# The first layer of a four-layer trunk: maxima moved ahead on VectorE, products with v in one piece, fewer mask operations, weight splits tied to the units

## The chip, the cores and the metric

One core of a Trainium2 chip runs the whole program. The metric is the device time of one execution in microseconds (us), from runs of the kernel on the chip. The engines are called PE (TensorE, matrix products; PEld is its weight load), DVE (VectorE), ACT (ScalarE), POOL (GpSimd) and SP (SyncE, which issues DMAs).

## The reference

A trunk of four layers over x, 256 tokens of width 1024, in float32. Each layer normalises its input, mixes tokens in its own way, gates, projects and adds the normalised result. The first layer is native sparse attention with 16 query heads in 4 groups, and only that layer is touched here:

```python
q, kc, vc, ks, vs, kw, vw, gl, z = split_cols(u @ w_in, A_SPLITS)
p_c = masked_softmax(einsum(qb, kcmp) - slopes * dist, dist >= 0)   # 15 compressed keys
o_c = einsum(p_c, vcmp)
p_s = masked_softmax(einsum(qb, ksel) - slopes * dist, dist >= 0)   # selected blocks
p_w = masked_softmax(einsum(qb, kwin) - slopes * dist, mask)        # window
o = sum(gates * stack([o_c, o_s, o_w]))
return (o * silu(z)) @ w_out
```

With 256 tokens the selection takes all four blocks and the window covers everything, so both branches are causal softmax over all keys.

## The kernel before, in words

**Weights.** All weight matrices come through one list, `seq`, of 512 KB pieces. `advance` (L69) issues their loads on SP's queue into five raw buffers and splits each piece in two: ACT writes `whi`, a rounded copy (L104), and DVE `wlo`, the rest (L106). Each projection step is then three matmuls (hi with hi, lo with hi, hi with lo: L200 to L202). There are 11 buffer pairs (`NH`). A piece is freed after its eight steps and `advance` is called again, so a new piece is split when one is freed. Splits are ranked 250 places later than their place in the program (`LATE`). `st["after"]` holds instructions behind which the splits must be issued on their engine, and `st["most"]` is an upper limit on the piece to be split.

**Order.** PE's order is written by hand. On the other engines the compile step picks the order by rank, with `tc.high_priority(offset=...)` moving an instruction ahead by so many places (negative: back); an engine then executes its instructions in that fixed order. `evac`, the copy from PSUM, has `EARLY` = 80.

**The units of the first layer.** Eight units (`nsa_unit`, L767), each for two query heads, run in a pipeline (`pipeline`, L368). A unit's front is `scores_of(0, (0, 1))`, `scores_of(1, (0,))` and `finish`; its back, run among the front of the next unit, is two sets of transposes (`trans`) and two sets of products with v (`pv`). Even units begin with `cmp_front`, the compressed branch of a group, and its transposes (`cmp_back`) come in the next unit. After each slot `fill` runs some projection steps, so that 97 of them (the rest of q, and z) are spread over the slots: two per slot as long as more steps than slots remain, then one. Eight are kept for the end.

**In a unit.** Scores go to two PSUM buffers `S` (L785, L786). `softmax` (L293) adds the mask and takes the row maximum in one DVE instruction (L294, which releases the score buffer), and ACT takes the exponential (L296). In `finish` the row sums are inverted (L797) and times the gate (L800), and DVE scales the eight blocks of weights (L806, L807). PE transposes them (L301), ACT copies them out of PSUM (L146), and PE multiplies with v in 64-column halves (L317, L320); the compressed products (L819) follow behind the second set, then the copy of `o` (L144 or L146). `cmp_front` takes a third use of the `S` buffers (L736), reduces it (L740), adds the mask in four operations (L743), multiplies by slopes in two (L746), and goes on through maximum, exponential and sum (L749 to L758).

Of the kernel before, what the change touches and what calls it, by code (L numbers as in the profile page):

```python
# [15 lines left out]
OP = mybir.AluOpType  # L16
# [6 lines left out]
BIG = 3e38  # L23
NH, NS = 11, 5
LATE, LATEZ, EARLY = -250, -60, 80
# [12 lines left out]
def trunk(ctx, tc, I, out):  # L38
    nc = tc.nc
    PE, ACT, DVE, POOL = nc.tensor, nc.scalar, nc.vector, nc.gpsimd  # L40
# [9 lines left out]
    seq = []  # L50
# [15 lines left out]
    st = {"load": 0, "split": 0, "next": 0, "held": 0, "parts": 0, "after": [], "most": len(seq)}  # L66
# [71 lines left out]
    def evac(dst, src, eng=None):  # L138
        if eng is None:
            eng = "va"[cnt["ev"] % 2]  # L140
            cnt["ev"] += 1
        with tc.high_priority(offset=EARLY):
            if eng == "v":
                DVE.tensor_copy(dst, src)  # L144
            else:
                ACT.activation(dst, src, AF.Copy)  # L146
# [144 lines left out]
        return v  # L291

    def softmax(S, mask, slope, c0, c1, P, mx, l):  # L293
        DVE.tensor_tensor_reduce(out=P[:, c0:c1], in0=S, in1=mask[:, c0:c1], scale=-slope, scalar=BIG,  # L294
                                 op0=OP.add, op1=OP.min, accum_out=mx)
        ACT.activation(P[:, c0:c1], P[:, c0:c1], AF.Exp, bias=mx, scale=-1.0, accum_out=l)  # L296

    def transpose_p(P, eng=None):
        pt = ps.tile([128, 4, 128], F32, name="pt", bufs=2)
# [68 lines left out]
    def pipeline(units, ga, pattern, keep=8, tail=3):  # L368

        n = len(units)  # L370
        order = []
        for i in range(n + 1):
            f = list(units[i][0]) if i < n else [lambda: None] * tail
            b = list(units[i - 1][1]) if i else []
            for x in pattern:
                src = f if x == "F" else b
                if src:
                    order.append(src.pop(0))
            order += f + b
            if i == n - 1:  # L380
                order.append(ga.open)
        plan["slots"], plan["keep"] = len(order), keep
        for f in order:
            f()
            fill()
        drain()
        assert ga.ready == 4
        return ga.gh
# [160 lines left out]
    causal = [mask_tile("causal") for _ in range(2)]  # L549
# [3 lines left out]
    SLA = slopes_of(16)  # L553
# [6 lines left out]
    slc = const.tile([128, 4, 4], F32, name="slc")  # L560
    for hd in range(16):
        POOL.memset(slc[:, hd // 4, hd % 4:hd % 4 + 1], SLA[4 * (hd // 4) + hd % 2])
    dcmp = const.tile([128, 2, 2, 15], F32, name="dcmp")
    d0 = dcmp[:, 0]
    POOL.iota(d0, pattern=[[-128, 2], [16, 15]], base=31, channel_multiplier=-1,
              allow_small_or_imprecise_dtypes=True)
    POOL.affine_select(out=d0, in_=d0, pattern=[[128, 2], [-16, 15]], base=-31, channel_multiplier=1,
                       fill=NEG, compare_op=OP.is_ge)
    POOL.tensor_scalar(dcmp[:, 1], d0, 0.5, None, op0=OP.mult)
    bm = const.tile([60, 4], F32, name="bm")  # L570
    POOL.memset(bm, 0.5)
    POOL.affine_select(out=bm, in_=bm, pattern=[[-15, 4]], base=0, channel_multiplier=1, fill=0.0,
# [75 lines left out]
    t = {}  # L648
# [22 lines left out]
    def hidden_t():  # L671
# [7 lines left out]
        for k in range(2):  # L679
# [3 lines left out]
    vbd = [v[0:60, g // 2, 512 + 256 * (g % 2):768 + 256 * (g % 2)].rearrange("p (a d) -> p a d", a=4)  # L683
           for g in range(4)]
# [20 lines left out]
    n = st["next"]  # L705
# [17 lines left out]
    qT = t["q"]  # L723

    ga = Gate(0.5, silu_tanh)
    ga.push()
    CS, PTC = {}, {}

    def cmp_front(g):

        need(g)
        sc = ps.tile([128, 512], F32, name="S", bufs=NSB)
        for b in range(2):
            for a in range(4):
                c0 = (b * 4 + a) * 32
                PE.matmul(sc[:, c0:c0 + 32], qT[:, 4 * g + a, b * 128:(b + 1) * 128],  # L736
                          kc[:, g].rearrange("p a b -> p (a b)"), start=True, stop=True)
        cs = CS[g] = work.tile([128, 2, 4, 15], F32, name="cs", bufs=2)
        two = sc[:, 0:256].rearrange("p (a s n) -> p a n s", s=2, n=16)[:, :, 0:15, :]
        DVE.tensor_reduce(out=cs.rearrange("p b a n -> p (b a) n"), in_=two, axis=AX.X, op=OP.add)  # L740
        for b in range(2):
            for c in range(2):
                DVE.tensor_tensor(cs[:, b, 2 * c:2 * c + 2], cs[:, b, 2 * c:2 * c + 2],  # L743
                                  dcmp[:, c, b, None, :].to_broadcast([128, 2, 15]), op=OP.add)
        for b in range(2):
            DVE.tensor_tensor(cs[:, b], cs[:, b], slc[:, g, :, None].to_broadcast([128, 4, 15]), op=OP.mult)  # L746
        cs8 = cs.rearrange("p b a n -> p (b a) n")
        cm, cl = small(8, "cm", 2), small(8, "cl", 2)
        DVE.tensor_reduce(out=cm, in_=cs8, axis=AX.X, op=OP.max)  # L749
        DVE.tensor_scalar(cm, cm, -1e20, None, op0=OP.max)  # L750
        DVE.tensor_tensor(cs8, cs8, cm[:, :, None].to_broadcast([128, 8, 15]), op=OP.subtract)
        ACT.activation(cs, cs, AF.Exp)
        DVE.tensor_reduce(out=cl, in_=cs8, axis=AX.X, op=OP.add)
        DVE.tensor_scalar(cl, cl, 1e-30, None, op0=OP.max)
        DVE.reciprocal(cl, cl)
        DVE.tensor_tensor(cl.rearrange("p (b a) -> p b a", b=2), cl.rearrange("p (b a) -> p b a", b=2),
                          gate[:, :, 4 * g:4 * g + 4], op=OP.mult)
        DVE.tensor_tensor(cs8, cs8, cl[:, :, None].to_broadcast([128, 8, 15]), op=OP.mult)  # L758
# [8 lines left out]
    def nsa_unit(p):  # L767
        g, i = divmod(p, 2)
        t = {}

        def start():
            need(g)
            t["P"] = {(j, br): work.tile([128, 384], F32, name="P", bufs=8) for j in range(2) for br in range(2)}
            t["l"], t["mx"] = small(8, "la", 3), small(8, "mxa", 3)

        def scores_of(b, js):
            if b == 0:
                start()
            n = 128 * (b + 1)
            S = {}  # L780
            for j in js:
                s = ps.tile([128, 512], F32, name="S", bufs=NSB)
                s = s[:, 0:2 * n].rearrange("p (a n) -> p a n", a=2)
                q = qT[:, 2 * p + j, b * 128:(b + 1) * 128]
                PE.matmul(s, q, KH[:, g, :, 0:n], start=True, stop=False)  # L785
                PE.matmul(s, q, KL[g // 2][:, g % 2, :, 0:n], start=False, stop=True)  # L786
                S[j] = s
            for j in js:
                for br in range(2):
                    x = (j * 2 + br) * 2 + b  # L790
                    softmax(S[j][:, br, :], causal[i], SLA[4 * g + j], 128 * b, 128 * b + n, t["P"][j, br],
                            t["mx"][:, x:x + 1], t["l"][:, x:x + 1])

        def finish():
            scores_of(1, (1,))
            l = t["l"]
            DVE.reciprocal(l, l)  # L797
            gv = bass.AP(tensor=gate.tensor, offset=gate.offset + 16 + 2 * p,
                         ap=[list(gate.ap[0]), [1, 2], [16, 2], [48, 2]])
            DVE.tensor_tensor(l.rearrange("p (j r b) -> p j r b", j=2, r=2),  # L800
                              l.rearrange("p (j r b) -> p j r b", j=2, r=2), gv, op=OP.mult)
            for br in range(2):
                for j in range(2):
                    x = (j * 2 + br) * 2
                    P = t["P"][j, br]
                    DVE.tensor_scalar(P[:, 0:128], P[:, 0:128], l[:, x:x + 1], None, op0=OP.mult)  # L806
                    DVE.tensor_scalar(P[:, 128:384], P[:, 128:384], l[:, x + 1:x + 2], None, op0=OP.mult)  # L807

        def trans(br):
            t["PT", br] = [transpose_p(t["P"][j, br], "a") for j in range(2)]  # L810

        def pv(br):
            if br == 0:
                t["o"] = ps.tile([128, 256], F32, name="o", bufs=1)
            o = t["o"]
            pv_pair(o, t["PT", br], v, (br * 256 + g * 64,) * 2, br == 0, False)
            if br == 1:
                for j in range(2):
                    PE.matmul(o[64 * j:64 * j + 64, :], vbd[g][:, 2 * i + j, :], PTC[g], start=False, stop=True)  # L819
                evac(ga.oT[:, p, :], o)  # L820
                ga.have_o(p)

        front = [lambda: scores_of(0, (0, 1)), lambda: scores_of(1, (0,)), finish]
        back = [lambda: trans(0), lambda: trans(1), lambda: pv(0), lambda: pv(1)]
        if i == 0:
            front.insert(0, lambda: cmp_front(g))
            back.insert(0, lambda: cmp_back(g))
        return front, back

    trans = out_proj(pipeline([nsa_unit(p) for p in range(8)], ga, "FFBFBBB"), 0)  # L830


    SLB = slopes_of(8)
# [10 lines left out]
    for i in range(2):  # L844
        DVE.tensor_tensor_reduce(out=ljunk, in0=lamt[:, 2 * i, :], in1=lamt[:, 2 * i + 1, :], scale=1.0,
                                 scalar=0.0, op0=OP.mult, op1=OP.add, accum_out=lam[:, i:i + 1])
# [24 lines left out]
    ga = Gate(0.5, silu_tanh)  # L871
# [280 lines left out]
```

## Time and profile before

| | us |
|---|---|
| median of 3 runs (lowest to highest) | 589.78 (587.52 to 589.93) |
| the profiled execution, its own time | 592.12 |
| its span, first to last instruction | 590.4 |
| PE busy, share of the span | 568.9, 96% |
| DVE busy | 420.6, 71% |
| ACT busy | 334.8, 57% |
| POOL busy | 40.7, 7% |

The profile's times are microseconds from the start of the span. A busy PE is not PE at its peak, as matmuls are pipelined. The share of an engine is a mean over stages that differ: the four layers each have a stage of attention units with projections between, and a stage of projections alone. The units of the first layer run from about 72 to 165 us.

### The profile page before, as it was taken

The numbers are of one execution on the slowest core, as the hardware profiler recorded it, in microseconds if no ns is written. First come the engines' busy times: TensorE is split into PE (matmuls) and PEld (weight loads), VectorE is DVE, ScalarE is ACT, GpSimd is POOL, SyncE is SP. The second block draws the span as 40 slices with busy tenths as digits, with TensorE's granted clock in tenths as the row PEclk, the third lists the DMA queues.
The fourth block names the chain that finished last, engine by engine and source line by source line (L and its number), as shares of the span: only waits on it lengthen the run. The fifth ranks groups of instructions, "written<-read, shape, count | busy, mean of one in ns | idle before, by whom it ended". The sixth has DMA issues, their size and how long they took to land.

```text
span 590.4 us, 10479 instructions
## 1 busy us (share of the span) xinstructions
PE 568.9 (96%) x3930; PEld 502.5 (85%) x3930; DVE 420.6 (71%) x947; ACT 334.8 (57%) x715; POOL 40.7 (7%) x89
## 2 busy tenths in 40 slices
PE   7999987999999999999999999999999999999995
PEld 6998876777788799999988789998987898998984
DVE  5983898877836886777965885656748768888622
ACT  5742787767825575577633473555724655756410
POOL 1900000000000100000410100000001000000000
PEclk9999998989999999999999999999999999999998
DMA  8774825521250596443451587433434683342012
GB/s 284 243 256 143 314 79 191 170 70 40 78 171 11 180 331 235 144 143 108 143 167 48 179 295 267 143 116 105 146 107 147 223 314 137 117 134 73 1 37 72
DMA packets 27779, 90.96 MB, mean 154 GB/s; under 512 B 4560, under 2 KB 5200, under 8 KB 27728
## 3 DMA queue, kind: packets, MB, share of 16 engines
q1 hardware_dynamic: 26144, 86.09, 42.9%
q10 hardware_dynamic: 1584, 4.20, 2.2%
q8 instruction: 31, 0.51, 0.4%
q14 instruction: 20, 0.16, 0.1%
HBM read 89.22 MB, written 1.05 MB: 153 GB/s over the span
## 4 chain that ended last, share of the span: by engine, by line
PE 81%; DVE 9%; issue 4%; ACT 2%; DMA 2%; POOL 1%; SPq 0%; POOLq 0%; DVEq 0%; ACTq 0%
PE mm L200 15%; PE mm L201 14%; PE mm L202 14%; PE mm L260 6%; PE mm L262 6%; PE mm L261 6%; PE S L311 4%; PE pt L301 3%; DVE wlo L106 3%; PE o L317 2%; PE o L655 1%; DVE P L294 1%; ACT whi L104 1%; DMA h<-in_x_dram 1%; PE pt L188 1%
## 5 line engine op out<-in xcount | busy, mean ns | idle before, releaser
L200 PE MATMUL mm<-uth,whi 128*128 128x256 f32 x736 | 219.8, 299 | 0.0
L106 DVE TENSOR_TENSOR wlo<-raw,whi 128x1024 fp32r<-128x1024 f32 (+1 forms) x153 | 182.2, 1206 | 42.8 <-ACT whi L104 42.1
L201 PE MATMUL mm<-utl,whi 128*128 128x256 f32 x736 | 208.4, 283 | 0.0
L202 PE MATMUL mm<-uth,wlo 128*128 128x256 f32 x736 | 208.2, 283 | 0.0
L104 ACT ACTIVATE whi<-raw 128x1024 fp32r<-128x1024 f32 (+1 forms) x153 | 157.3, 1045 | 82.3 <-PE mm L201 50.0
L200 PEld LDWEIGHTS mm<-uth,whi 128*128 128x128 f32 x736 | 141.0, 192 | 17.5 <-issue 16.7
L201 PEld LDWEIGHTS mm<-utl,whi 128*128 128x128 f32 x736 | 141.4, 192 | 0.9
L202 PEld LDWEIGHTS mm<-uth,wlo 128*128 128x128 f32 x736 | 141.0, 192 | 0.0
L260 PE MATMUL mm<-whi,qT 128*128 128x512 f32 x128 | 50.4, 394 | 0.0
L261 PE MATMUL mm<-whi,kT 128*128 128x512 f32 x128 | 49.9, 390 | 0.0
L262 PE MATMUL mm<-wlo,qT 128*128 128x512 f32 x128 | 49.9, 390 | 0.0
L260 PE MATMUL mm<-whi,uth 128*128 128x512 f32 (+1 forms) x112 | 42.5, 380 | 0.0
L262 PE MATMUL mm<-wlo,uth 128*128 128x512 f32 (+1 forms) x112 | 42.1, 376 | 0.0
L261 PE MATMUL mm<-whi,utl 128*128 128x512 f32 (+1 forms) x112 | 42.0, 375 | 0.0
L294 DVE CUSTOM_DVE_ANT_0 P<-S,mask 128x128 f32<-128x128 f32 (+1 forms) x96 | 30.6, 353 | 8.4 <-PE S L786 6.2
L415 ACT ACTIVATE junk<-mm 128x512 bf16<-128x512 f32 x16 | 9.5, 595 | 42.1 <-PE mm L262 42.1
L296 ACT ACTIVATE P<-P,mxa 128x128 f32<-128x128 f32 (+1 forms) x64 | 28.5, 448 | 4.1 <-DVE mxa L294 4.1
L146 ACT ACTIVATE PT<-pt 128x384 f32<-128x384 f32 x58 | 26.1, 484 | 8.2 <-PE pt L301 7.9
L301 PE MATMUL pt<-ident,P 128*128 128x128 f32 x180 | 28.0, 286 | 0.5 <-DVE P L806 0.4
L262 PEld LDWEIGHTS mm<-wlo,qT 128*128 128x128 f32 x128 | 24.0, 188 | 5.1
L260 PEld LDWEIGHTS mm<-whi,qT 128*128 128x128 f32 x128 | 24.1, 188 | 4.7
L261 PEld LDWEIGHTS mm<-whi,kT 128*128 128x128 f32 x128 | 24.1, 188 | 4.6
(207 smaller groups left out, 768.8 us busy)
## 6 DMA issues: line engine op xcount, KB each, us to landing
raw<-in_a_t_dram SPq DMA_DIRECT2D x24, 512.0 KB, 4.9
raw<-in_b_t_dram SPq DMA_DIRECT2D x24, 512.0 KB, 4.6
raw<-in_d_t_dram SPq DMA_DIRECT2D x24, 512.0 KB, 4.8
raw<-in_c_t_dram SPq DMA_DIRECT2D x20, 512.0 KB, 4.6
raw<-in_w_dram SPq DMA_DIRECT2D x8, 512.0 KB, 4.8
raw<-in_a_o_dram SPq DMA_DIRECT2D x8, 512.0 KB, 3.5
raw<-in_b_v_dram SPq DMA_DIRECT2D x8, 512.0 KB, 3.5
raw<-in_b_o_dram SPq DMA_DIRECT2D x8, 512.0 KB, 3.5
```

Source lines behind the costliest of these rows:

```text
L104: ACT.activation(hi, t, AF.Copy)
L106: lo_of = (POOL if on_pool else DVE).tensor_tensor(lo, t, hi.bitcast(F32), op=OP.subtract)
L146: ACT.activation(dst, src, AF.Copy)
L200: PE.matmul(o, sh, mh, start=first, stop=False)
L201: PE.matmul(o, sh, ml, start=False, stop=False)
L202: PE.matmul(o, sl, mh, start=False, stop=last)
L260: PE.matmul(o, sh, wh[:, j, c0:c1], start=k == 0, stop=False)
L261: PE.matmul(o, sl, wh[:, j, c0:c1], start=False, stop=False)
L262: PE.matmul(o, sh, wl[:, j, c0:c1], start=False, stop=k == 7)
L294: DVE.tensor_tensor_reduce(out=P[:, c0:c1], in0=S, in1=mask[:, c0:c1], scale=-slope, scalar=BIG, op0=OP.add, op1=OP.min, accum_out=mx)
L296: ACT.activation(P[:, c0:c1], P[:, c0:c1], AF.Exp, bias=mx, scale=-1.0, accum_out=l)
L301: PE.transpose(pt[:, i, :], P[:, i * 128:(i + 1) * 128], ident)
```

## The change

- `softmax` returns its DVE instruction. In the first layer it is called with `EARLY`, so the maximum and the exponential rank 80 places earlier.
- The two sets of products with v become one slot, `pvs`, with the compressed products behind; the pattern of the slots loses a B.
- The mask of the compressed branch is stored in another order of its axes, and four additions and two multiplications become one of each, over 120 columns.
- `finish` sets `st["after"]` to its last maximum, raises the limit on pieces to be split and calls `advance`. The limit starts at 42 and is 42 + 2p after unit p; after the last unit there is none.

```diff
     def softmax(S, mask, slope, c0, c1, P, mx, l):
-        DVE.tensor_tensor_reduce(out=P[:, c0:c1], in0=S, in1=mask[:, c0:c1], scale=-slope, scalar=BIG,
-                                 op0=OP.add, op1=OP.min, accum_out=mx)
+        top = DVE.tensor_tensor_reduce(out=P[:, c0:c1], in0=S, in1=mask[:, c0:c1], scale=-slope, scalar=BIG,
+                                       op0=OP.add, op1=OP.min, accum_out=mx)
         ACT.activation(P[:, c0:c1], P[:, c0:c1], AF.Exp, bias=mx, scale=-1.0, accum_out=l)
+        return top.ins
...
     ga = Gate(0.5, silu_tanh)
+    PACE = st["most"] = st["next"] + 2
     ga.push()
...
-        for b in range(2):
-            for c in range(2):
-                DVE.tensor_tensor(cs[:, b, 2 * c:2 * c + 2], cs[:, b, 2 * c:2 * c + 2],
-                                  dcmp[:, c, b, None, :].to_broadcast([128, 2, 15]), op=OP.add)
-        for b in range(2):
-            DVE.tensor_tensor(cs[:, b], cs[:, b], slc[:, g, :, None].to_broadcast([128, 4, 15]), op=OP.mult)
+        pairs = cs.rearrange("p b (c j) n -> p (b c) j n", j=2)
+        DVE.tensor_tensor(pairs, pairs, dcmp.rearrange("p b c n -> p (b c) n")[:, :, None, :]
+                          .to_broadcast([128, 4, 2, 15]), op=OP.add)
+        DVE.tensor_tensor(cs, cs, slc[:, g, None, :, None].to_broadcast([128, 2, 4, 15]), op=OP.mult)
...
-                    softmax(S[j][:, br, :], causal[i], SLA[4 * g + j], 128 * b, 128 * b + n, t["P"][j, br],
-                            t["mx"][:, x:x + 1], t["l"][:, x:x + 1])
+                    with tc.high_priority(offset=EARLY):
+                        st["max"] = softmax(S[j][:, br, :], causal[i], SLA[4 * g + j], 128 * b, 128 * b + n,
+                                            t["P"][j, br], t["mx"][:, x:x + 1], t["l"][:, x:x + 1])
 
         def finish():
             scores_of(1, (1,))
+            st["after"], st["most"] = [st["max"]], PACE + 2 * p if p < 7 else len(seq)
+            advance()
...
-            if br == 1:
-                for j in range(2):
-                    PE.matmul(o[64 * j:64 * j + 64, :], vbd[g][:, 2 * i + j, :], PTC[g], start=False, stop=True)
-                evac(ga.oT[:, p, :], o)
-                ga.have_o(p)
+
+        def pvs():
+            pv(0)
+            pv(1)
+            o = t["o"]
+            for j in range(2):
+                PE.matmul(o[64 * j:64 * j + 64, :], vbd[g][:, 2 * i + j, :], PTC[g], start=False, stop=True)
+            evac(ga.oT[:, p, :], o)
+            ga.have_o(p)
...
-        back = [lambda: trans(0), lambda: trans(1), lambda: pv(0), lambda: pv(1)]
+        back = [lambda: trans(0), lambda: trans(1), pvs]
...
-    trans = out_proj(pipeline([nsa_unit(p) for p in range(8)], ga, "FFBFBBB"), 0)
+    trans = out_proj(pipeline([nsa_unit(p) for p in range(8)], ga, "FFBFBB"), 0)
+    st["after"] = []
```

## Rows read from the trace of the kernel before

**Rows 1.** The page, busy time of each engine, its share and instructions.
```profile
PE 568.9 (96%) x3930; PEld 502.5 (85%) x3930; DVE 420.6 (71%) x947; ACT 334.8 (57%) x715; POOL 40.7 (7%) x89
```

**Rows 2.** Windows; busy per engine (PE, PEld, DVE, ACT, POOL), clock, DMA.
```profile
70.00:110.00 40.00, 33.74 (x253) 29.30 (x251) 35.98 (x131) 31.36 (x82) 0.00 (x0) 0.96 0.47 159
110.00:125.00 15.00, 13.82 (x99) 11.84 (x97) 12.74 (x57) 10.18 (x32) 0.00 (x0) 0.89 0.32 107
125.00:165.00 40.00, 38.84 (x296) 30.19 (x295) 30.83 (x133) 29.12 (x91) 1.16 (x4) 1.00 0.22 70
...
100.00:105.00 5.00, 5.00 (x34) 4.34 (x35) 4.18 (x10) 3.92 (x10) 0.00 (x0) 0.74 0.41 121
120.00:125.00 5.00, 4.88 (x28) 4.77 (x28) 3.58 (x26) 3.05 (x12) 0.00 (x0) 0.69 0.01 4
```

**Rows 3.** PE's timeline, score products and a transpose; brackets: idle before, releaser.
```profile
75.63 0.47 PE L785 MATMUL S<-kT,qT 128*128 128x512 f32 x1 [1.49 <-DVE cm L750]
...
77.54 0.47 PE L785 MATMUL S<-kT,qT 128*128 128x512 f32 x1 [0.51 <-DVE cl L754]
...
93.34 0.39 PE L785 MATMUL S<-kT,qT 128*128 128x256 f32 x1 [0.93 <-DVE cs L740]
...
98.70 0.47 PE L785 MATMUL S<-kT,qT 128*128 128x512 f32 x1 [2.78 <-DVE cm L750]
...
120.12 0.58 PE L785 MATMUL S<-kT,qT 128*128 128x256 f32 x1 [1.09 <-DVE cs L740]
...
133.16 1.05 PE L301 MATMUL pt<-ident,P 128*128 128x128 f32 x5 [0.21 <-DVE P L806]
```

**Rows 4.** DVE's timeline ahead of PE's longest stall.
```profile
92.89 0.40 DVE L740 TENSOR_REDUCE cs<-S 128x120 f32<-128x240 f32 x1
...
95.94 1.23 DVE L106 TENSOR_TENSOR wlo<-raw,whi 128x1024 fp32r<-128x1024 f32 x1
97.09 0.48 DVE L743 TENSOR_TENSOR cs<-cs,dcmp 128x30 f32<-128x30 f32 x4
...
97.86 0.29 DVE L294 CUSTOM_DVE_ANT_0 P<-S,mask 128x128 f32<-128x128 f32 x1
...
98.27 0.28 DVE L294 CUSTOM_DVE_ANT_0 P<-S,mask 128x128 f32<-128x128 f32 x1
```

**Rows 5.** PE's timeline, the products with v of units 2 and 5.
```profile
114.20 0.65 PE L317 MATMUL o<-PT,v 128*64 128x256 f32 x4
...
144.09 0.65 PE L317 MATMUL o<-PT,v 128*64 128x256 f32 x4
...
144.89 0.39 PE L200 MATMUL mm<-uth,whi 128*128 128x256 f32 x1
145.11 0.28 PE L201 MATMUL mm<-utl,whi 128*128 128x256 f32 x1
145.23 0.28 PE L202 MATMUL mm<-uth,wlo 128*128 128x256 f32 x1
145.44 0.65 PE L317 MATMUL o<-PT,v 128*64 128x256 f32 x4
...
146.24 0.65 PE L819 MATMUL o<-PTc,v 60*64 60x256 f32 x4
```

**Rows 6.** ACT's timeline, an exponential and the last copy of transposed weights.
```profile
114.02 0.50 ACT L296 ACTIVATE P<-P,mxa 128x256 f32<-128x256 f32 x1
...
114.52 0.48 ACT L146 ACTIVATE PT<-pt 128x384 f32<-128x384 f32 x1
```

**Rows 7.** DVE's timeline ahead of the scalings of unit 3.
```profile
117.05 0.43 DVE L144 COPY oT<-o 128x256 f32<-128x256 f32 x1 [0.77 <-PE o L819]
```

**Rows 8.** Groups by line and shape, DVE, 71 to 165 us; xcount, busy us, mean ns.
```profile
L106 DVE TENSOR_TENSOR wlo<-raw,whi 128x1024 fp32r<-128x1024 f32 x18 | 21.6, 1214 | 0.0
L294 DVE CUSTOM_DVE_ANT_0 P<-S,mask 128x256 f32<-128x256 f32 x32 | 12.7, 416 | 4.5 <-PE S L786 4.5
...
L751 DVE TENSOR_TENSOR cs<-cs,cm 128x120 f32<-128x120 f32 x4 | 1.1, 280 | 0.0
```

More of the change, by code (lines that the diff above doesn't have):

```diff
@@ L563, in trunk @@
     dcmp = const.tile([128, 2, 2, 15], F32, name="dcmp")
-    d0 = dcmp[:, 0]
+    d0 = dcmp[:, :, 0]
     POOL.iota(d0, pattern=[[-128, 2], [16, 15]], base=31, channel_multiplier=-1,
@@ L568, in trunk @@
                        fill=NEG, compare_op=OP.is_ge)
-    POOL.tensor_scalar(dcmp[:, 1], d0, 0.5, None, op0=OP.mult)
+    POOL.tensor_scalar(dcmp[:, :, 1], d0, 0.5, None, op0=OP.mult)
     bm = const.tile([60, 4], F32, name="bm")
```

## The prediction

> **What bounds the kernel now.** I began with the page's busy shares: PE is busy for 568.9 of 590.4 us [rows 1], so all that a change off PE can give back is the 21.5 us in which PE stands still, the stretches in which PE's clock is halved, and work that PE does needlessly. Next I cut the stage that the diff touches, the eight units of the first layer (70 to 165 us), into windows [rows 2]. The reader is to see three regimes. From 70 to 110 PE is busy for 33.74 of 40 us while DVE is busy for 35.98: DVE has no room, and PE pays. From 110 to 125 PE loses 1.18 us, and the mean clock is 0.89. From 125 on PE is busy for 38.84 of 40 at a clock of 1.00, so there is about 1 us left to win. The clock has two levels here, 2.4 and 1.2 GHz, and a mean of 0.74 or 0.69 over 5 us [rows 2] means lost work of 0.26 x 5 = 1.3 us and 0.31 x 5 = 1.55 us. Both stretches come right behind a stall of PE.
>
> Then PE's timeline: the stalls of this stage are waits of the score products (L785) for a free score buffer [rows 3]. There are two such buffers; one comes free when both maxima that read it (L294) are through, or, behind the compressed products, when the reduction L740 is. DVE's own timeline shows why the longest stall (2.78 us, until 98.70) lasts so long [rows 4]: L740 frees the second buffer at 93.3 and the products of this unit's scores follow from 93.34 on [rows 3], but their maxima stand in DVE's queue behind eight scalings of the unit before (L806/L807), a q split (L644), a weight split (L106 at 95.94, 1.23 us) and six mask operations (L743/L746 from 97.09); the first runs at 97.86, the second at 98.27, and PE goes on at 98.70. PE's row names L750 as releaser, a tiny operation that stands between the maxima.
>
> **The change, part by part.**
>
> Products with v. pv(1) now follows pv(0) with no projection steps between. At 144.09 the first product starts, at 144.89 a projection step, at 145.44 the second product, whose successor L819 starts at 146.24 [rows 5]. A product set thus takes 0.80, and the gap of 1.35 between the two starts is 0.80 plus 0.55 for three matmuls; at full pace they take 0.36, as 256-column matmuls follow each other by 0.12 (145.11 and 145.23). So 0.19 us is the price of going from 64-column to 128-column work and back. All eight units pay it: 8 x 0.19 = **1.5 us** of PE, which nothing hides. The steps themselves move elsewhere.
>
> Fillers. The order has 60 slots instead of 68, for the same 97 projection steps, 8 of them kept back. Counted through, the units get 8, 14, 14, 14, 11, 7, 7, 8 (and 6 behind the last) instead of 8, 16, 16, 9, 8, 8, 8, 9 (7): unit 3, the one ahead of the second half-clock stretch, gains five steps. PE's total is the same; I put nothing on it.
>
> Pacing. Pieces 42 and later may now be split only when a unit's finish has raised the limit. Counted through the code this never binds: with 11 buffers, piece 42 can't be split before the 33rd projection step, in unit 2, when the limit is 44 already; 43 comes in unit 3 under 46, and so on. What is left is that the DVE half of a split is ordered behind the last maximum of the latest finished unit. It is an order on one queue, without a new semaphore, and the split already stands 250 places late. Cost and gain 0; no DMA is moved, and SP's and POOL's queues keep their order. If it did delay a split, eleven pieces of cover stand ahead of it.
>
> Mask operations. Six become two, four times. The six take 0.77 us (97.09 to 97.86 [rows 4]). A 128x120 operation of this kind (L751) has 280 ns [rows 8], so two of them take 0.56 at the most, and some 0.4 if they overlap as the six do (estimate). That frees 4 x 0.37 = 1.5 us of DVE. Once the maxima go first it is on no path of PE: 0, with 1.5 as the far end.
>
> Maxima first. Maximum and exponential rank 80 places earlier, ahead of scalings, q splits and mask operations.
> - Unit 0: stalls of 1.49 and 0.51 [rows 3]. Two maxima and one tiny operation take 0.41 (97.86 to 98.27 [rows 4]), so four in a row are through in some 0.85, while PE has two projection steps (0.72) to run before it asks. I take 2.0; bounds 0 and 2.0.
> - Unit 2: the stall of 2.78 [rows 3] goes, since the maxima no longer wait until 97.86, and with it the half clock behind it, 1.3 [rows 2]: 4.1. The 0.93 before it waits for L740, which keeps its rank: 0 taken, 0.93 as far end.
> - Unit 4: 1.09 [rows 3], again L740, which stands behind the scalings of unit 3, and these behind a copy for which DVE waited 0.77 [rows 7]; then 1.55 of half clock. The scalings of unit 3 can come earlier when their maxima do, but the copy may still block them: half of 2.6, **1.3**; bounds 0 and 2.6.
> - From unit 4's end on PE's waits are a few tenths each, 1.16 in all from 125 to 165 [rows 2], with DVE idle: they stay.
>
> What gets late instead: the scalings. In units 1, 3, 5 and 7 the transposes of the unit before follow finish directly, and in unit 5 PE already waits 0.21 for a scaling [rows 3]. Two 256-column maxima ahead of them are up to 2 x 0.42 = 0.83 [rows 8]. On ACT the exponentials (0.50) get ahead of the copies of the transposed weights; the last copy of unit 2 starts at 114.52 and ends at 115.00 [rows 6], which is just when the joined second product would start (114.20 + 0.80 [rows 5]), so that cover has no slack there. Bounds: 0 and 4 x (0.83 + 0.50) = 5.3. I take 0.9, near the low end, because the only such wait that the trace shows is 0.21.
>
> Sum: 1.5 + 2.0 + 4.1 + 1.3 - 0.9 = **8.0 us**. The profiled execution took 592.12 (span 590.4), 2.3 above the median of 589.78; taken off that, 584.1, and on the median's scale **581.8**.
>
> **Rivals.**
> 1. DVE bounds the first stretch. It has 4.0 us idle in 70 to 110. If everything on it must be done in order, the stretch shrinks by the merged operations alone, 2 x 0.37, and with the products the gain is 2.2: 587.6. For it: 90% busy. Against: 18 weight splits, 21.6 us of the stage's DVE time [rows 8], are needed only eleven pieces later and can slide into 110 to 165. Chance 0.12.
> 2. The half clock stays or moves. The runs of 64-column work grow longer, and a stall of 1.09 was enough before [rows 2, 3]. Two new stretches at 1.5 each leave a gain of 5: 584.8; with a third, 586.3. Chance 0.12.
> 3. Slower: an early maximum whose scores have not come holds up the scalings behind it, as the copy at 117.05 held up L797 [rows 7]; the transposes come late in every unit. At the far end of 5.3 for the odd units, the same 1.33 for the three even ones (4.0), and two half-clock stretches (3.1), 12.4 stands against 1.5 + 2.0 + 4.1 = 7.6: 594.6. It decides once a unit's transposes wait for more than 8.9/7 = 1.3 us. The Trainium skill says the same in "TensorE: Matmul & The Clock Gate" (Part 1, Architectural detail): ACT and DVE are strict first-in-first-out, so whatever is put ahead blocks what is ready behind it. By that rule alone every early maximum is a risk; the trace agrees that the queue blocks, in the 0.77 of that copy. Chance 0.08.
> 4. The pacing, by its name, should do something. By the count it doesn't; were it to bind, it would only thin out DVE in the first units, the way of the forecast. No chance of its own.
>
> **How the numbers follow.** The forecast case has the remaining 0.68. The range goes from 577.2, where unit 2 gives its 0.93, unit 4 its other 1.3 and the masks their 1.5 as well, and the late scalings cost nothing (8.0 + 0.93 + 1.3 + 1.5 + 0.9 = 12.6), to 587.6, which is rival 1. It leaves out rival 3 and some tails, under 0.2. This kernel's measurement tells 0.5% from no change, so faster means below 586.8: all of the forecast case, most of rival 2, a quarter of rival 1: 0.80. Same takes the rest of these, 0.12; slower is rival 3, 0.08.
>
> **What would show it.** Right: L294 in front of L806 and L743 in DVE's timeline; no stall of PE over 1 us at unit 0 and 2; clock 1.00 from 95 to 105; the products' starts 0.80 apart in all units; splits at the same steps as before. Wrong: transposes (L301) with waits for L806 of over a microsecond, PE waiting for the copies L146 ahead of the second product, or a clock under 0.9 in a new place. The forecast falls if PE's idle time in the stage stays near the 8.6 us of now [rows 2].

## The result and the profile after

The changed kernel takes 595.2 us (median of 4 runs, 593.02 to 598.96) against 589.28 for the kernel before (587.52 to 589.93, 4 runs): ratio 1.0116, 95% interval 1.009 to 1.0141. It is **slower**, by some 1.2%, and the forecast of 581.8, faster, was wrong. The profiled execution took 598.96 us (span 597.2), the longest of the four. Of all runs reported below one stands far apart and unexplained, 1663.4 us, one of six of the kernel that comes out fastest: its median of 582.41 counts that run, its ratio doesn't, and the median of the other five is 581.9.

One statement ahead of the prediction has to be corrected first. The limit on splits starts at 34, not at 42, and is 34 + 2p after unit p: the line that takes `st["next"] + 2` stands ahead of `ga.push()`, which takes eight pieces more. The pacing therefore does bind, which the prediction denies.

The page of the kernel after, busy time by engine, beside [rows 1]:

```profile
PE 569.7 (95%) x3930; PEld 504.4 (84%) x3930; DVE 422.1 (71%) x931; ACT 333.5 (56%) x715; POOL 40.6 (7%) x89
```

No engine's busy time grew by more than 1.9 us (PE's weight load); DVE lost 16 instructions, the merged mask operations. So the time is in waits and in the clock. The windows of the kernel after (columns as in [rows 2]); the last row is the whole stage, from the first compressed product to the first matmul of the out-projection:

```profile
70.00:110.00 40.00, 31.07 (x230) 27.33 (x228) 30.15 (x109) 28.37 (x74) 0.00 (x0) 0.87 0.33 119
110.00:125.00 15.00, 14.75 (x119) 13.11 (x119) 14.26 (x57) 10.32 (x33) 0.00 (x0) 1.00 0.24 73
125.00:165.00 40.00, 34.52 (x237) 26.96 (x235) 29.39 (x120) 28.16 (x92) 1.15 (x4) 0.91 0.24 81
...
80.00:90.00 10.00, 3.75 (x16) 3.55 (x17) 9.90 (x21) 5.01 (x9) 0.00 (x0) 0.58 0.51 171
...
140.00:150.00 10.00, 10.00 (x72) 8.12 (x72) 7.35 (x30) 5.28 (x18) 0.00 (x0) 0.85 0.19 57
...
160.00:165.00 5.00, 5.00 (x34) 3.65 (x32) 3.56 (x12) 3.32 (x7) 0.00 (x0) 0.66 0.34 116
...
71.00:174.45 103.45, 89.11 (x652) 75.26 (x652) 80.80 (x300) 69.69 (x202) 1.15 (x4) 0.92 0.28 97
```

And the same stage of the kernel before, in one window:

```profile
71.08:167.55 96.47, 88.20 (x652) 73.26 (x652) 79.69 (x316) 71.34 (x203) 1.16 (x4) 0.96 0.33 108
```

The stage grew by 103.45 - 96.47 = 6.98 us, and the two profiled executions differ by 598.96 - 592.12 = 6.84: between these two the whole loss is here (the medians differ by 5.92). PE's idle time went from 96.47 - 88.20 = 8.27 to 103.45 - 89.11 = 14.34, 6.07 of the 6.98. PE's busy time rose by 0.91 although its products got shorter (below), since more of it ran at the lower clock (mean 0.92 against 0.96).

Which work waits is plain from the groups by line of this stage (busy, mean ns | idle before them and what ended it). Before:

```profile
L301 PE MATMUL pt<-ident,P 128*128 128x128 f32 x96 | 15.6, 298 | 0.5 <-DVE P L806 0.4
...
L785 PE MATMUL S<-kT,qT 128*128 128x256 f32 (+1 forms) x32 | 11.8, 370 | 7.8 <-DVE cm L750 4.3 <-DVE cs L740 2.0 <-DVE mxa L294 0.9
```

After (the transposes of the weights are now L302, those of the mask L763):

```profile
L302 PE MATMUL pt<-ident,P 128*128 128x128 f32 x96 | 16.3, 306 | 6.2 <-DVE P L809 3.6 <-ACT PT L146 2.4
...
L785 PE MATMUL S<-kT,qT 128*128 128x256 f32 (+1 forms) x32 | 11.4, 361 | 1.1 <-DVE mxa L294 1.0
...
L763 PE MATMUL pt<-ident,cs 128*60 128x128 f32 x8 | 1.7, 306 | 7.0 <-DVE cs L758 7.0
```

The reader is to see an exchange. The scores' waits fell from 7.8 to 1.1 us, as forecast. In their place transposes wait: 7.0 us for the mask chain, once, and 6.2 for scalings and for copies of transposed weights. PE's timeline after has the places:

```profile
86.25 0.60 PE L763 MATMUL pt<-ident,cs 128*60 128x128 f32 x2 [7.00 <-DVE cs L758]
...
93.82 0.92 PE L302 MATMUL pt<-ident,P 128*128 128x128 f32 x6 [1.34 <-ACT PT L146]
...
136.97 1.16 PE L302 MATMUL pt<-ident,P 128*128 128x128 f32 x6 [2.03 <-DVE P L809]
...
139.28 1.28 PE L302 MATMUL pt<-ident,P 128*128 128x128 f32 x6 [0.79 <-ACT PT L146]
...
158.81 1.32 PE L302 MATMUL pt<-ident,P 128*128 128x128 f32 x6 [1.57 <-DVE P L809]
```

How the 7.00 comes about is read on two engines. In the kernel before, DVE's subtraction of the mask chain, ACT's exponential and DVE's last operation of that chain ran at

```profile
75.68 0.28 DVE L751 TENSOR_TENSOR cs<-cs,cm 128x120 f32<-128x120 f32 x1
...
76.32 0.29 ACT L752 ACTIVATE cs<-cs 128x120 f32<-128x120 f32 x1
...
78.63 0.28 DVE L758 TENSOR_TENSOR cs<-cs,cl 128x120 f32<-128x120 f32 x1
```

After, on ACT, that exponential stands behind ten early exponentials of the softmax, of which these are the first and the last:

```profile
76.00 0.49 ACT L296 ACTIVATE P<-P,mxa 128x256 f32<-128x256 f32 x1
...
80.00 0.49 ACT L296 ACTIVATE P<-P,mxa 128x256 f32<-128x256 f32 x1
...
80.49 0.29 ACT L752 ACTIVATE cs<-cs 128x120 f32<-128x120 f32 x1
```

and on DVE, after:

```profile
78.21 0.23 DVE L751 TENSOR_TENSOR cs<-cs,cm 128x120 f32<-128x120 f32 x1
...
79.27 0.28 DVE L809 TENSOR_SCALAR P<-P,la 128x128 f32<-128x128 f32 x1
...
81.10 0.27 DVE L753 TENSOR_REDUCE cl<-cs 128x8 f32<-128x120 f32 x1
81.29 1.22 DVE L106 TENSOR_TENSOR wlo<-raw,whi 128x1024 fp32r<-128x1024 f32 x1
...
83.53 1.17 DVE L106 TENSOR_TENSOR wlo<-raw,whi 128x1024 fp32r<-128x1024 f32 x1
84.62 0.16 DVE L756 TENSOR_TENSOR cl<-cl,gate 128x8 f32<-128x8 f32 x1
84.69 1.22 DVE L106 TENSOR_TENSOR wlo<-raw,whi 128x1024 fp32r<-128x1024 f32 x1
85.83 0.28 DVE L758 TENSOR_TENSOR cs<-cs,cl 128x120 f32<-128x120 f32 x1
```

The exponential's input is ready at 78.21 + 0.23 = 78.44 and it runs at 80.49: 2.05 us behind other exponentials. Then the tiny operations of the chain find three weight splits among them (3.61 us). The chain ends 7.2 us later than before (85.83 against 78.63). Counted from each stage's start (71.08 before, 71.00 after), the subtraction L751 runs 2.61 later, the exponential 4.25 and the end of the chain 7.28: 2.61 arise on DVE ahead of the subtraction, where the early maxima now stand, 1.64 on ACT, and 3.03 behind the exponential, where the splits are. DVE is busy for 9.90 of the 10 us from 80 to 90: it is not short of work, it does the wrong work first. The mean clock of that window is 0.58.

The 2.03 of unit 5 has the same look on DVE, after. Sums are inverted at 132.84; a split, four early maxima (the first is shown) and a second split stand ahead of the first scaling:

```profile
132.84 0.20 DVE L800 RECIPROCAL la<-la 128x8 f32<-128x8 f32 x1
...
132.96 1.17 DVE L106 TENSOR_TENSOR wlo<-raw,whi 128x1024 fp32r<-128x1024 f32 x1
134.05 0.42 DVE L294 CUSTOM_DVE_ANT_0 P<-S,mask 128x256 f32<-128x256 f32 x1
...
135.51 1.22 DVE L106 TENSOR_TENSOR wlo<-raw,whi 128x1024 fp32r<-128x1024 f32 x1
136.64 0.28 DVE L809 TENSOR_SCALAR P<-P,la 128x128 f32<-128x128 f32 x1
```

That the pacing binds is seen in the windows of the splits alone (L106; columns DVE, POOL, clock, DMA share, GB/s), before:

```profile
96.00:112.00 16.00, 5.98 (x5) 0.00 (x0) 0.89 0.43 136
```

and after, where no piece is split for 16 us, and the DMA moves next to nothing:

```profile
96.00:112.00 16.00, 0.00 (x0) 0.00 (x0) 1.00 0.00 2
```

### The profile page after: what moved, and what is told of

It reads as the page before. It is cut to its first block, busy times and chain, and to the rows that moved or that the text cites. A ratio compares the mean times of both kernels' runs of the same rounds, so it can differ in the third digit from the quotient of the medians.

```text
span 597.2 us, 10456 instructions
## 1 busy us (share of the span) xinstructions
PE 569.7 (95%) x3930; PEld 504.4 (84%) x3930; DVE 422.1 (71%) x931; ACT 333.5 (56%) x715; POOL 40.6 (7%) x89
## 4 chain that ended last, share of the span: by engine, by line
PE 81%; DVE 8%; issue 4%; ACT 2%; DMA 2%; POOL 1%; SPq 0%; POOLq 0%; DVEq 0%; ACTq 0%
PE mm L200 15%; PE mm L201 14%; PE mm L202 14%; PE mm L260 6%; PE mm L262 6%; PE mm L261 6%; PE S L312 4%; PE pt L302 4%; DVE wlo L106 3%; PE o L318 2%; DVE P L294 1%; PE o L656 1%; DMA h<-in_x_dram 1%; ACT whi L104 1%; PE o L321 1%
## 5 line engine op out<-in xcount | busy, mean ns | idle before, releaser
L106 DVE TENSOR_TENSOR wlo<-raw,whi 128x1024 fp32r<-128x1024 f32 (+1 forms) x153 | 182.3, 1206 | 41.6 <-ACT whi L104 41.0
L294 DVE CUSTOM_DVE_ANT_0 P<-S,mask 128x128 f32<-128x128 f32 (+1 forms) x96 | 29.1, 354 | 11.6 <-PE S L786 9.1
L302 PE MATMUL pt<-ident,P 128*128 128x128 f32 x180 | 28.7, 290 | 6.2 <-DVE P L809 3.6
L146 ACT ACTIVATE PT<-pt 128x384 f32<-128x384 f32 x58 | 25.6, 480 | 7.8 <-PE pt L302 7.6
L302 PEld LDWEIGHTS pt<-ident,P 128*128 128x128 f32 x180 | 21.5, 147 | 8.6 <-DVE P L809 4.0
```

What stands on the lines that cost most here:

```text
L106: lo_of = (POOL if on_pool else DVE).tensor_tensor(lo, t, hi.bitcast(F32), op=OP.subtract)
L294: top = DVE.tensor_tensor_reduce(out=P[:, c0:c1], in0=S, in1=mask[:, c0:c1], scale=-slope, scalar=BIG, op0=OP.add, op1=OP.min, accum_out=mx)
L302: PE.transpose(pt[:, i, :], P[:, i * 128:(i + 1) * 128], ident)
```

## The experiments

Theory A: the early rank of the softmax pushes back what PE needs next (mask chain, scalings, copies). Theory B: the pacing moves the splits to bad places. Each edit is against the kernel named; where an edit repeats one shown, it is only named. Ratios are to the kernel before on the same chip; between the chips the median of the kernel before differs by up to 0.65 us (589.28 to 589.93), so differences of medians below are good to about that. "Stage" is the stretch defined above, 96.47 us before and 103.45 after.

### Taking the change apart

**The rank alone, on the kernel before.**

```diff
-                    softmax(S[j][:, br, :], causal[i], SLA[4 * g + j], 128 * b, 128 * b + n, t["P"][j, br],
+                    with tc.high_priority(offset=EARLY):
+                        softmax(S[j][:, br, :], causal[i], SLA[4 * g + j], 128 * b, 128 * b + n, t["P"][j, br],
...
```

> The kernel before with the early rank of maxima and exponentials alone. Theory A (rank): the early rank by itself makes the compressed mask chain and the scalings late, so PE waits 7 us for the transposes of the mask in unit 1 and 1.5 to 2 us for scalings in units 5 and 7: some 595, slower than 589.3. Theory B (pacing): the losses come from the limit on splits, which starts at 34 and binds; the early rank alone removes stalls as forecast: 583 to 585.

Measured: 594.3 us, 1.0065 [1.0039, 1.0092], stage 98.93 with 11.99 idle. PE's timeline of this kernel has waits of the same two kinds:

```profile
83.31 0.38 PE L763 MATMUL pt<-ident,cs 128*60 128x128 f32 x2 [3.29 <-DVE cs L758]
...
111.44 1.16 PE L301 MATMUL pt<-ident,P 128*128 128x128 f32 x6 [2.58 <-DVE P L807]
```

This one edit, to which the prediction gave 7.4 - 0.9 = 6.5 of its 8.0 us, loses by itself, as theory A expected. The mask's wait is 3.29 here and not the 7 expected; the scalings' longest are 2.58, 1.24 and 1.19.

**The products alone, on the kernel before** (`pvs` and the pattern "FFBFBB", as in the diff of the change).

> The kernel before with the joined products with v alone. Both theories: 0.19 us saved in each of eight units, 1.5 us, 587.8; starts of the two product sets 0.70 to 0.80 apart. If the new spread of projection steps matters, it shows here as more than 1 us off that.

Measured: 589.99, 0.9999 [0.9979, 1.0018]. The 587.8 expected did not come. In the stage PE is busy for 84.11 us, 4.1 less than before, in part because more of it ran at the full clock (mean 0.98 against 0.96), and idle for 11.27, 3.0 more: the scores wait for DVE (2.82, 1.66, 1.52 and 1.49 at the four worst places). By the medians nothing is left of PE's saving where DVE sets the pace.

**The change without the rank.**

```diff
-                    with tc.high_priority(offset=EARLY):
-                        st["max"] = softmax(S[j][:, br, :], causal[i], SLA[4 * g + j], 128 * b, 128 * b + n,
+                    st["max"] = softmax(S[j][:, br, :], causal[i], SLA[4 * g + j], 128 * b, 128 * b + n,
...
```

> The changed kernel without the early rank: pacing, joined products and merged mask operations stay. Theory A (rank): the 7 us wait of unit 1 goes, and the time comes to 587 to 589. Theory B (pacing): the splits still come in pairs behind each unit's last maximum, and most of the loss stays: 592 to 595.

Measured: 588.88, 0.9984 [0.9964, 1.0004], stage 94.84. Without the rank the change is not slower than the kernel before; 6.3 us lie between this and the changed kernel.

**The change without the pacing.**

```diff
-    PACE = st["most"] = st["next"] + 2
...
-            st["after"], st["most"] = [st["max"]], PACE + 2 * p if p < 7 else len(seq)
-            advance()
```

> The changed kernel without the limit on splits and without their order behind the maxima. Theory A (rank): the wait in unit 1 stays, since the order of DVE there is the same up to the mask chain's end: 592 to 595. Theory B (pacing): 583 to 587.

Measured: 594.05, 1.0074 [1.0045, 1.0103]. The wait of the mask's transposes is still 7.01 us. Theory B falls as the main cause; theory A stands. In the window in which the changed kernel splits nothing, this one splits three pieces (L106 alone, columns as above), so the gap there does come from the pacing:

```profile
96.00:112.00 16.00, 3.60 (x3) 0.00 (x0) 1.00 0.30 105
```

### Which of the pushed-back work matters

**The mask chain early too**, in the changed kernel: all of `cmp_front` from the reduction on.

```diff
+        with tc.high_priority(offset=EARLY):
             cs = CS[g] = work.tile([128, 2, 4, 15], F32, name="cs", bufs=2)
...
```

> The changed kernel with the whole mask chain (reduction to last product, DVE and ACT) given the same early rank as the maxima. Theory A1 (the chain was pushed back): PE's wait of 7 us in unit 1 goes and with it the half clock behind it; the waits for scalings in units 5 and 7 stay: 586 to 589. Rival A2 (the 7 us come from the weight splits that stand in the chain's way, and would stand elsewhere): PE waits as long for scalings in unit 1, and the time stays at 593 to 596.

Measured: 592.83, 1.0072 [1.0049, 1.0095]. The 7.00 us wait is gone; PE's timeline shows who is late instead:

```profile
83.70 1.59 PE L302 MATMUL pt<-ident,P 128*128 128x128 f32 x6 [3.17 <-DVE P L810]
```

The time lies between the two expectations: with the chain's 7.00 gone, the medians differ by only 2.4 us.

**The scalings early as well** (on top of the last one).

```diff
+            with tc.high_priority(offset=EARLY):
                 l = t["l"]
                 DVE.reciprocal(l, l)
...
```

> As e5, and the scalings with their reciprocal and gate early too, so only q splits, copies of z and weight splits are late. Theory A1: the waits for scalings in units 5 and 7 (3.6 us) go as well: 582 to 586. Rival (the queue only moves its wait to the copies and q splits): no better than e5.

Measured: 586.15, 0.995 [0.9934, 0.9966]. Now the kernel is faster than before, and 6.7 us under the last one on the same chip. The longest waits that remain are for copies of transposed weights on ACT (0.84, 1.26, 1.88).

**Only the maxima early**, in the changed kernel: the exponentials keep their rank.

```diff
-    def softmax(S, mask, slope, c0, c1, P, mx, l):
-        top = DVE.tensor_tensor_reduce(
+    def softmax(S, mask, slope, c0, c1, P, mx, l, early=0):
+        with tc.high_priority(offset=early):
+            top = DVE.tensor_tensor_reduce(
...
```

> The changed kernel with the early rank on the maxima alone; the exponentials go back to their own place. If ACT's exponentials ahead of the mask's exponential make the chain late (it ran at 80.5, behind ten of them), the 7 us wait falls to 3 or less and the time to 589 to 592. If the maxima on DVE do it, the wait and the time stay: 593 to 596.

Measured: 590.83, 1.0025 [1.001, 1.0041]. The wait of the mask's transposes shrinks, but does not go:

```profile
83.01 0.60 PE L764 MATMUL pt<-ident,cs 128*60 128x128 f32 x2 [4.33 <-DVE cs L759]
```

So 2.67 of the 7.00 go with the rank of the exponentials. Yet hardly any of it was spent in ACT's queue. The chain's exponential on ACT and its end on DVE are here

```profile
79.77 0.29 ACT L753 ACTIVATE cs<-cs 128x120 f32<-128x120 f32 x1
...
82.58 0.28 DVE L759 TENSOR_TENSOR cs<-cs,cl 128x120 f32<-128x120 f32 x1
```

Counted from the stage's start (70.42 here), the exponential runs at 9.35, against 9.49 in the changed kernel (it waits less behind others, but the subtraction ahead of it runs at 8.49 instead of 7.21), and the chain ends at 12.16, against 14.83. What the exponentials' rank changed is DVE's order behind the exponential: one split now stands among the chain's last operations instead of three. The wait is longer than the 3 us expected, but the time is in the range that went with it: by the medians, 4.4 of the 5.9 us that the change lost go with the exponentials' rank.

**All three early, without the pacing** (the edits that make the mask chain and the scalings early, and the one without pacing).

> As e6 without the limit on splits and without their order behind the maxima. If pacing costs something (e4 was 1 us under the changed kernel, inside its spread), this is 1 to 2 us below e6; if it spaces the splits well, above.

Measured: 585.57, 0.9939 [0.9918, 0.996], stage 90.21, mean clock 1.00. Its longest wait:

```profile
107.26 0.92 PE L302 MATMUL pt<-ident,P 128*128 128x128 f32 x6 [1.88 <-ACT PT L146]
```

### What the other parts are worth, on the last kernel

**Its products apart again** (four slots in a unit's back, "FFBFBBB").

> As e8, but the two products with v apart again, with projection steps between. If the joined products give their 0.19 us in each of eight units, this is 1.5 us above e8: 587.1. If what they save comes back as a wait for the copies L146, as e2 alone (no gain) suggests, it is equal to e8 within 0.5 us, or below it.

Measured: 587.65, 0.9956 [0.993, 0.9983]; 2.1 us above the last kernel by the medians, with intervals that overlap.

**Its mask operations six again.**

> As e8, but with the six mask operations of before. If the 1.5 us of DVE that the merging frees lie on PE's path in the first units, where DVE is full, this is up to 1.5 us above e8; if not, equal within 0.5 us.

Measured: 585.79, 0.9947 [0.9919, 0.9975]: 0.2 from the last kernel. On this kernel the merged operations are worth nothing that can be measured; the two intervals are 2.5 and 3.3 us wide, so 1.5 is not excluded.

**Its maxima and exponentials back at their own rank**; mask chain and scalings stay early (the edit of the third experiment).

> As e8, but maxima and exponentials at their own rank; mask chain and scalings stay early. If early maxima bring anything once nothing is put behind them (the stalls of 2.0 in unit 0 and 2.78 and 1.3 in unit 2), this is 3 to 5 us above e8: 588.5 to 590.5. If the gain of e8 came from the scalings and the mask chain, it is equal to e8 within 1 us.

Measured: **582.41, 0.9874 [0.9833, 0.9915]**, the fastest of all by the medians, 12.8 us under the changed kernel. Neither expectation came: it is 3.2 us below the last kernel. Its waits of over half a microsecond are the scores' again (these and one of 0.65), and its mean clock in the stage is 1.00. PE's timeline:

```profile
73.09 0.47 PE L785 MATMUL S<-kT,qT 128*128 128x512 f32 x1 [1.21 <-DVE mxa L294]
...
92.69 0.47 PE L785 MATMUL S<-kT,qT 128*128 128x512 f32 x1 [1.64 <-DVE mxa L294]
...
100.73 0.36 PE L785 MATMUL S<-kT,qT 128*128 128x256 f32 x1 [0.92 <-DVE mxa L294]
```

and its first window, beside [rows 2]:

```profile
70.00:110.00 40.00, 35.59 (x280) 30.97 (x279) 38.92 (x140) 35.41 (x98) 0.00 (x0) 1.00 0.44 144
```

DVE is busier than in any of the others (38.92 of 40), and PE gets 280 matmuls through instead of 253 (274 instead of 247 when both are counted over 40 us from the start of their own stage). The queue is as full as before; what stands first in it is different.

**The kernel with all early, and its copies of transposed weights 80 places earlier.**

```diff
...
-        evac(t.rearrange("p (a b) -> p a b", a=3), pt[:, 0:3, :], eng)
+        with tc.high_priority(offset=early):
+            evac(t.rearrange("p (a b) -> p a b", a=3), pt[:, 0:3, :], eng)
...
-            t["PT", br] = [transpose_p(t["P"][j, br], "a") for j in range(2)]
+            t["PT", br] = [transpose_p(t["P"][j, br], "a", EARLY) for j in range(2)]
```

> As e8, with the copies of the transposed weights another 80 places earlier, ahead of the exponentials. e8's largest waits of PE are for these copies (1.88, 0.84, 0.81, 1.09 us); if the exponentials ahead of them are the cause, 2 to 4 us below e8: 582 to 584. If the scalings before the transposes are what is late, equal to e8.

Measured: 583.08, 0.989 [0.9854, 0.9926]: 2.5 under the same kernel without it, in the range expected if early exponentials had pushed these copies back, though the two intervals overlap by a little. PE's longest wait for the copies fell from 1.88 to 0.89. Early maxima and exponentials with all of this moved as well are thus within the noise of the fastest kernel, which leaves them where they were.

**The fastest kernel with that edit.**

> As e11, with the copies of the transposed weights 80 places earlier as in e12. If both gains are of different waits, 579.5 to 581; if e11 has already taken what e12 took (PE's waits for L146 are gone in e11 but for 0.48 us), equal to e11 within 0.7 us.

Measured: 582.99, 0.9882 [0.9861, 0.9903]. Nothing more: with exponentials at their own rank the copies are not late.

**The fastest kernel with its mask chain at its own rank.**

> As e11 with the scalings (and their reciprocal and gate) early, the mask chain at its own rank. If the scalings carry the gain, equal to e11 within 1 us (582 to 583.5); if the mask chain does, back at 587 to 589.

Measured: 583.92, 0.9907 [0.9887, 0.9926]. It is 3.8 us under the same kernel without any early rank, run on the same chip (587.69, below): the scalings carry most of the gain.

### The price of the pacing

**No early rank at all and no pacing** (the kernel before with joined products and merged mask operations), beside the change without the rank; and **the fastest kernel with the pacing**.

> Joined products and merged mask operations on the kernel before; no pacing, no early rank. e3, the same with pacing, took 588.9. If pacing costs time by itself, this is 1 to 3 us below e3: 586 to 588; if pacing helps or does nothing, 588.5 to 590.

> As e11 (mask chain and scalings early, maxima at their own rank), with the limit on splits and their order put back. If pacing costs time, 1 to 3 us above e11: 583.5 to 585.5; if not, equal within 1 us.

Measured: 587.69, 0.9962 [0.9946, 0.9978], against 588.88 with pacing; and 584.85, 0.9916 [0.9899, 0.9932], against 582.41 without. With the two pairs further up (595.2 and 594.05; 586.15 and 585.57) the pacing costs 1.2, 2.4, 1.15 and 0.6 us: four times the same sign, each time with intervals that overlap. That it costs about a microsecond is likely; whether through the limit or through the order behind the last maximum was not tried.

The kernel of 587.69 differs from the one with the products alone (589.99, 0.9999 [0.9979, 1.0018]) by the merged mask operations only, and it is 2.3 us faster, with intervals that just miss each other, on different chips. Without early maxima the merged operations thus seem to be worth something; with them (the kernel with six mask operations above) nothing was seen.

## Why the prediction was wrong, point by point

- **What bounds the kernel** was read rightly: DVE has no room from 70 to 110 [rows 2]. But on a full engine with a fixed order, what goes first makes something else late, here by 12.7 us of PE's waits against the 6.7 that went. The prediction did not follow that through.
- **The failed step** is the term for what gets late, 0.9 in the sum: it measured 12.7, of which 7.0 are the mask chain and 5.7 the transposes of the weights. The chain was left out by the sentence in the part on mask operations that "Once the maxima go first it is on no path of PE: 0". The mask chain is on a path: PE transposes its result in the next unit (`cmp_back`). That was in the kernel's description, yet it was missing in the list of "what gets late instead", which held the scalings and the copies only. It made one wait of 7.00 us. That is not its price in time: cured alone it gave back 2.4 us by the medians, since transposes of the weights then waited 3.17 for scalings, and cured together with the scalings 9.05. The exponentials were counted against ACT's copies and not against the chain; by the medians their rank alone goes with 4.4 us.
- **The late scalings** were named rightly and mis-sized: 0.9 taken, with 5.3 as the far end. The transposes' waits, copies included, rose from 0.5 to 6.2, by 5.7, past the far end. The row I leaned on, a wait of 0.21 [rows 3], was taken in the order that the change undoes; it says nothing of the order after. The nearest fair row was the far end.
- **Maxima first:** the mechanism worked at every place named. The stalls of 1.49, 0.51, 2.78 and 1.09 [rows 3] are gone, and the scores' idle time fell by 6.7. In unit 0 four maxima in a row take the 0.85 that the prediction gives (73.15 to 74.00 on DVE, after), but by luck: the 0.41 from 97.86 to 98.27 [rows 4] is the time from the start of one maximum to the start of the next, with a tiny operation between, and not two maxima. The half clock was not won, it moved: to 80 to 90 (0.58), 140 to 150 (0.85) and 160 to 165 (0.66), in part what rival 2 had said. That the longer runs of 64-column work bring it, as that rival supposes, no run shows: with all early the products are joined and the stage has a mean of 1.00.
- **Products:** 0.19 a unit was too small. After, PE's timeline shows

```profile
117.76 0.65 PE L318 MATMUL o<-PT,v 128*64 128x256 f32 x4
...
118.46 0.60 PE L318 MATMUL o<-PT,v 128*64 128x256 f32 x4
...
119.21 0.65 PE L826 MATMUL o<-PTc,v 60*64 60x256 f32 x4
```

  so from the first set to the compressed products it takes 1.45, against 146.24 - 144.09 = 2.15 less one step of 0.36, 1.79, before [rows 5]: 0.34 a unit, and 2.7 in eight if all are alike (an estimate). I had assumed that a joined set still takes 0.80; it takes 0.70 to 0.75. The larger saving showed as time only once DVE's order was mended (2.1 by the medians, with overlapping intervals); on the kernel before it came to nothing.
- **Pacing:** 0 rested on a limit read eight pieces too high. The price is likely some 1 us.
- **Mask operations, fillers:** 0 for the merged operations, given for early maxima, agrees with what was measured there (585.57 against 585.79), and without early maxima they seem to be worth 2.3. The fillers were not tried by themselves.
- **The rivals:** the time landed at rival 3, 594.6, by luck in part. Its picture, an early instruction that holds up ready ones, was seen, with 2.05 us for the chain's exponential on ACT. The Trainium skill states in "TensorE: Matmul & The Clock Gate" (Part 1, Architectural detail) that the queues of ACT and DVE are strictly first-in-first-out; the trace agrees, with these 2.05 us. Yet the work held up most was not the scalings of every unit, as rival 3 had it, but one mask chain, beside scalings in units 5 and 7; and most of it was held up by work that ran, not by work that waited: 3.61 us of splits, and maxima whose scores had come. 0.08 was too little for a case with a full queue and rows of its own.

- **The signs named** as wrong came: transposes that wait over a microsecond for scalings, a clock under 0.9 in new places, and waits for the copies L146, though ahead of transposes (1.34 and 0.79) and not of the second product. The one that would make the forecast fall, idle time that stays near 8.6, was passed: it rose to 14.34 in the stage, from 8.27.

What stays open: why the fixed order put three splits among the chain's last operations. It is not the pacing, as without it three splits stand at the same places of the order (80.55, 82.78 and 83.95 on DVE); with the exponentials at their own rank one is left there. No run moved the splits alone.

## What to carry to other kernels

On an engine that is full and runs in a fixed order, moving an instruction ahead is an exchange: list everything that it passes, on every queue that it uses, with the next consumer of each, before any gain is counted. Here it paid to put the scalings first (583.92, and 582.41 with the mask chain), and not the maxima that PE was seen to wait for (594.3); early maxima did no harm once all that they passed was moved as well (583.08). And count a limit from the value that its variable has on the line where it is taken.

## What was unexpected in the hardware

- A wait of PE does not always bring the lower clock. A wait of 1.09 us was followed by a mean of 0.69 over 5 us before [rows 2, 3]; in the fastest kernel one of 1.64, and in the kernel with all early one of 1.88, left the mean of the stage at 1.00. What makes the difference was not tried.
- From the start of a set of products of 64 columns to the start of what follows it takes 0.70 and 0.75 us when the sets are joined, and 0.80 both times when a projection step stands between them [rows 5].
